# A two-layer hybrid attention trunk: weight blocks loaded two blocks ahead, measured on two engines, and the first x tiles normalised through PE

## The chip, the cores and the metric

The kernel runs on one core of a Trainium2 chip. A time is the device time of one execution in microseconds (us), and the time of a kernel is the median of its runs. Five engines work beside each other, each through its own instructions in their order: PE (matrix multiplications; "PEld" is the loading of its stationary operand), DVE (vector engine), ACT (scalar engine), POOL (GpSimd) and SP (which here only issues DMA transfers). An instruction that waits for data holds up everything behind it on its engine, and only that.

## What is computed

One sequence of 1024 rows, 1024 features and 16 heads of 64 goes through two layers of the form x + W_out(mixer(RMSNorm(x)) * silu(gate)). Layer 0 is causal attention with a forget gate ("fox"), layer 1 is windowed attention at three dilations, merged by a softmax over their log-sums ("dsw").

```python
D_MODEL, SEQ, DEPTH, HEAD_DIM, N_HEADS = 1024, 1024, 2, 64, 16
DSWA_GROUPS = ((128, 1), (512, 4), (2048, 16))      # window, dilation

def rms_norm(x, g):
    return x * lax.rsqrt(jnp.mean(x * x, axis=-1, keepdims=True) + EPS) * g

def fox_mixer(h, w_in, b_f, q_g, k_g):
    # proj = h @ w_in: q, k, v, gate of 1024 columns each, and 16 forget logits
    q, k = rms_norm(q, q_g), rms_norm(k, k_g)       # by head
    c = jnp.cumsum(jax.nn.log_sigmoid(f_logit + b_f), axis=1)
    # s = q k^T / 8 + c[query] - c[key], causal; o = softmax(s) v
    return o, gate

def dsw_mixer(h, cos, sin, w_in, q_g, k_g):
    # proj = h @ w_in: q, k, v for 3 groups x 16 heads (9216 columns) and a gate (1024)
    # q, k: rms_norm by head, rotary on 16 of the 64 features
    # per group: attention inside its window on every r-th row; o_g and lse_g
    return sum(softmax(lse over groups) * o_g), gate

# layer: x = x + (o * silu(gate)) @ w_out
```

## The kernel before

**Tiles and precision.** The 1024 rows are 8 tiles of 128. Every large product is made of three fp16 matmuls: an operand is held as a high and a low half, and high x high, high x low and low x high are summed. `xh`, `xl` hold the normalised input of a layer, turned so that its features lie on the partitions, and `yh`, `yl` the gated output of the mixer. The fp32 weights come from memory in 44 blocks of mostly 1024 x 384: 3 gate blocks, 8 fox blocks (q, k and v of two heads), 3 output blocks of layer 0; then 3 gate blocks, 24 dsw blocks (8 of dilation group 0, then groups 2 and 1 in turn), 3 output blocks of layer 1.

**One block's weights** (class `Weights`). A block is four pieces of 2 x 384 columns on 128 partitions, and four steps are done to each: `load` (a DMA on SP's queue into one of four `raw` buffers), `bound` (L270: DVE takes the largest absolute value of each partition, `vm`), `scale` (once per block: PE's small matmul L248 adds the squares of these over the partitions, and a chain of one-column operations on DVE makes a power of two `sw` of it, with `eps` and the factors `col`, `vs` for v), and `split` into the fp16 halves `w`. The split has two forms: on ACT and DVE (L300, L301: the high half by ACT, the remainder by DVE) or on POOL with a cast on ACT (L303, L304, L305). Pieces 1 and 3 go the first way, pieces 0 and 2 the second.

**Order.** PE's order is the order in which the program is written: for each of the eight tiles of a block `project` (L328, 24 matmuls into one of three `pj` buffers in PSUM), with attention work of earlier tiles between. The clock of that order is `Flow`: `project` ticks four times a tile, so a block has 32 ticks, and `flow.at(slot, ...)` writes a piece of work at a tick. `Weights.ahead()` puts the work on the next block into the present one: loads at ticks 2, 4, 6 and 9, bounds at 8, 10, 12, 15, the scale at 20, splits at 21, 23, 25, 27. On the other engines a scheduler arranges the instructions when the program is built; the ticks only tell it where a piece of work may begin. At run time each engine and SP's queue keep that fixed order.

**One tile after its projection.** DVE multiplies q and k by their gains out of `pj` (`u`, L410), ACT squares them (L415), ACT and DVE move v out as fp16 halves (`vt`, L420, L421); for each pair of tiles DVE makes the norms (L428, L451, L452, L454), ACT and POOL split q and k into halves (`hl`, L456, L457), and SP issues the transposing DMA into `qk_t` (L462). PE makes scores `s` (L482) from it, DVE and ACT the probabilities `p`, ACT and POOL their halves `ph` (L528, L531 in fox), another transposing DMA makes `ptt`, and PE multiplies with v (L539).

**Start.** x comes in twice: turned (`xt`, L554) and by rows (`xrow`). `row_factor` (L563 to L570) gets 1/rms of a tile's rows on ACT and DVE from the rows, puts it on a diagonal `dg`, and `split_xt` lets PE spread it over the partitions (L578) and multiplies and splits the turned tile. `load_gbc` reads the norm's gains as one row for every partition and takes their largest for the scale `sx`. The loads stand on SP's queue in the order row 0, gains, x 0, weights 0 and 1, gains as rows, weights 2 and 3, row 1, x 1, row 2, x 2.

Of the kernel before, what the change touches and what calls it, by code (L numbers as in the profile page):

```python
# [22 lines left out]
P = 128  # L23
D = 1024
# [12 lines left out]
CB = 2  # L37
PARTS = ((0, 384), (384, 256), (640, 384))
# [44 lines left out]
def trunk(ctx, tc, ins, out, cfg):  # L83
# [59 lines left out]
    xh, xl, yh, yl = (const.tile([P, KT, S], F16, name=n) for n in ("xh", "xl", "yh", "yl"))  # L143
# [81 lines left out]
    sx = const.tile([P, 2], F32, name="sx")  # L225
    sy = const.tile([P, 2], F32, name="sy")
# [8 lines left out]
    def root_floor(e, q, lo, hi):  # L235

        nc.vector.tensor_scalar(e, q, 1, 0x7FC00000, ALU.logical_shift_right, ALU.bitwise_and)
        nc.vector.tensor_scalar(e, e, float(127 << 22), None, ALU.add)
        nc.vector.tensor_single_scalar(e, e, 0x7F800000, ALU.bitwise_and)
        nc.vector.tensor_scalar(e, e, float((127 + lo) << 23), float((127 + hi) << 23), ALU.max, ALU.min)  # L240

    def spread_sums(src, n):
# [7 lines left out]
        nc.vector.tensor_reduce(v1, ws, AX.X, ALU.add)  # L250
        return v1
# [4 lines left out]
    class Weights:  # L256


        def __init__(self, src, n, layer, kind):
            self.src, self.n, self.layer, self.kind = src, n, layer, kind  # L260
            self.raw, self.pairs = {}, {}
            self.vm = sm.tile([P, KT // 2], F32, name="vm", tag="vm")
            self.vm2 = sm.tile([P, KT // 2], F32R, name="vm2", tag="vm2")

        def load(self, i):
            self.raw[i] = w_p.tile([P, 2, 384], F32, name="raw", tag="raw", bufs=4)
            nc.sync.dma_start(self.raw[i][:, :, : self.n], self.src[:, 2 * i : 2 * i + 2, :])

        def bound(self, i):
            nc.vector.tensor_reduce(self.vm[:, i : i + 1], self.raw[i][:, :, : self.n], AX.XY, ALU.max, apply_absolute_value=True)  # L270
            if i == KT // 2 - 1:
                nc.vector.tensor_mul(self.vm2, self.vm, self.vm)

        def scale(self):

            v1 = spread_sums(self.vm2, KT // 2)
            e = v1.bitcast(I32)
            root_floor(e, e, -16, 40)
            f = self.f = sm.tile([P, 6], F32, name="ws_f", tag="ws_f")
            sw, t2, inv = (f[:, i : i + 1] for i in range(3))  # L280
            self.sw, self.inv = sw, inv
            nc.vector.tensor_scalar(sw.bitcast(I32), e, -1.0, float(268 << 23), ALU.mult, ALU.add)  # L282
            by = sy if self.kind == "out" else sx
            nc.vector.tensor_mul(t2, sw, by[:, self.layer : self.layer + 1])
            nc.vector.reciprocal(inv, t2)
            if self.kind != "qkv":
                return
            self.eps, self.col, self.vs = (f[:, i : i + 1] for i in range(3, 6))
            nc.vector.scalar_tensor_tensor(self.eps, t2, EPS, t2, ALU.mult, ALU.mult)
            nc.vector.tensor_scalar(self.col, t2, 2.0 ** -15, 2.0 ** -14, ALU.mult, ALU.max)  # L290
            nc.vector.tensor_scalar(self.col, self.col, 2.0 ** 15, None, ALU.min)
            nc.vector.tensor_mul(self.vs, self.col, inv)
            lw = low[:, self.layer : self.layer + 1]
            nc.vector.tensor_tensor(lw, lw, sw, ALU.min)

        def split(self, i, own=False):
            raw, n = self.raw[i][:, :, : self.n], self.n
            w = self.pairs[i] = w_p.tile([P, 2, 2, 384], F16, name="w", tag="w", bufs=cfg["wbufs"])
            if own or (cfg["wl"][self.layer] >> i) & 1:
                nc.scalar.activation(w[:, 0, :, :n], raw, AF.Copy, scale=self.sw)  # L300
                nc.vector.scalar_tensor_tensor(w[:, 1, :, :n], raw, self.sw, w[:, 0, :, :n], ALU.mult, ALU.subtract)  # L301
            else:
                nc.gpsimd.tensor_scalar(raw, raw, self.sw, None, ALU.mult)  # L303
# [6 lines left out]
        def ahead(self):  # L310

            s0 = flow.now
            for i in range(KT // 2):
                flow.at(s0 + cfg["wload"][i], lambda i=i: self.load(i))
# [834 lines left out]
```

## Time and profile before

| | |
|---|---|
| median of 3 runs | 1936.68 us (1935.25 to 1941.52) |
| profiled execution | 1936.61 us |
| its span, first to last instruction | 1934.7 us |
| mean granted TensorE clock | 0.953 |
| busy: PE, DVE | 1688.3 (87%), 1318.4 (68%) |
| busy: POOL, ACT | 1081.7 (56%), 1010.9 (52%) |
| DMA engines, bytes moved by the queues | 66.4%, 292.54 MB on the hardware queue |

A span's busy time says how much an engine worked, not whether its work was waited for; for that the profile lists the idle time in front of an instruction and what ended it ("53.4 <- DMA" reads: 53.4 us of idle time that a DMA's landing ended). Lines in it such as `L270 DVE TENSOR_REDUCE vm<-raw` name the line of the kernel, the engine, the operation, and the program's names of what is written and read. The stages can be told by time: PE's first projection starts at 32.3 us, the fox blocks take some 60 us each, the 24 dsw blocks some 41 us each.

### The profile page before, as it was taken

How to read it: one execution, taken by the hardware profiler on the slowest of the kernel's cores; microseconds unless marked ns; L12 is line 12 of the kernel's file. 1: busy time of each engine (PE TensorE's matmuls, PEld its weight loads, DVE VectorE, ACT ScalarE, POOL GpSimd, SP SyncE). 2: the span in 40 equal slices, each digit the busy share in tenths (PEclk: the TensorE clock that was granted, in tenths of full speed). 3: DMA queues.
4: the chain of work that ended last, by engine and by line, in shares of the span. 5: the costliest groups of instructions: out<-in, count | busy, mean ns of one | idle time of the engine just before them, and what ended most of it. 6: DMA issues, size and time to landing. Idle time of an engine off the chain costs nothing.

```text
span 1934.7 us, 38039 instructions
## 1 busy us (share of the span) xinstructions
PE 1688.3 (87%) x13308; PEld 1071.8 (55%) x13308; DVE 1318.4 (68%) x4089; ACT 1010.9 (52%) x2492; POOL 1081.7 (56%) x1105
## 2 busy tenths in 40 slices
PE   3898888988888888998999989998988889998889
PEld 2655565655665434755666555555555555555544
DVE  8776676666756668676666686666766766767762
ACT  5545566555665445545555565544554554554620
POOL 4324566455654463255667656666676666767531
PEclk9999999988989998999999999999999999999999
DMA  7244977889879767246667686576565756567752
GB/s 250 93 159 97 186 172 152 162 169 182 167 147 193 207 207 220 89 122 138 130 138 141 143 189 132 133 146 130 132 134 140 165 129 139 139 145 149 184 160 88
DMA packets 659344, 294.96 MB, mean 152 GB/s; under 512 B 510272, under 2 KB 622912, under 8 KB 659152
## 3 DMA queue, kind: packets, MB, share of 16 engines
q1 hardware_dynamic: 659152, 292.54, 66.4%
q8 instruction: 104, 1.70, 0.4%
q14 instruction: 88, 0.72, 0.1%
HBM read 126.45 MB, written 41.22 MB: 87 GB/s over the span
## 4 chain that ended last, share of the span: by engine, by line
PE 25%; DMA 17%; DVE 15%; issue 5%; ACT 5%; POOL 4%; SPq 1%; DVEq 0%; ACTq 0%; POOLq 0%
PE pj L328 17%; DMA qk_t<-hl 6%; DMA raw<-in_w_dsw 6%; PE pj L352 5%; DVE w L301 3%; DMA ptt<-ph 2%; PE s L482 2%; DVE vm L270 2%; DVE p L943 1%; DMA og_d<-og 1%; ACT p L944 1%; DVE pj L428 1%; DVE u L410 1%; DMA raw<-in_w_do 1%; DVE u L454 1%
## 5 line engine op out<-in xcount | busy, mean ns | idle before, releaser
L328 PE MATMUL pj<-w,xh 128*128 128x384 f16 (+2 forms) x4864 | 1212.9, 334 | 55.5 <-DVE vt L421 43.3
L328 PE MATMUL pj<-w,xl 128*128 128x384 f16 (+2 forms) x2432 | 809.8, 333 | 9.2 <-DVE xl L864 7.8
L328 PEld LDWEIGHTS <-xh 128*128 128x128 f16 x4864 | 480.4, 101 | 353.6 <-issue 90.0
L328 PEld LDWEIGHTS <-xl 128*128 128x128 f16 x2432 | 244.4, 101 | 180.8 <-issue 23.7
L531 POOL TENSOR_TENSOR ph<-p,ph 128x512 f16<-128x512 f32 (+3 forms) x176 | 175.1, 1012 | 189.6 <-ACT ph L528 157.5
L303 POOL TENSOR_SCALAR raw<-raw,ws_f 128x768 f32<-128x768 f32 (+2 forms) x86 | 184.2, 2151 | 116.1 <-DVE ws_f L282 113.2
L482 PE MATMUL s<-qk_t 128*128 128x128 f16 (+1 forms) x1504 | 168.2, 255 | 91.6 <-DMA qk_t<-hl 82.8
L457 POOL TENSOR_TENSOR hl<-u,hl 128x512 f16<-128x512 f32 x128 | 151.6, 1184 | 164.6 <-ACT hl L456 145.3
L270 DVE TENSOR_REDUCE vm<-raw 128x1 f32<-128x768 f32 (+2 forms) x176 | 161.7, 921 | 100.1 <-DMA raw<-in_w_dsw 71.1
L415 ACT ACTIVATE sq<-pj 128x256 f32<-128x256 f32 x256 | 96.8, 378 | 225.5 <-DVE u L410 214.3
L949 POOL TENSOR_TENSOR ph<-p,ph 128x768 f16<-128x768 f32 (+2 forms) x96 | 153.8, 1602 | 87.3 <-ACT ph L948 85.5
L482 PEld LDWEIGHTS <-qk_t 128*128 128x128 f16 x1504 | 117.3, 101 | 110.8 <-DMA qk_t<-hl 91.5
L352 PE MATMUL pj<-yh,w 128*128 128x512 f16 x512 | 161.8, 386 | 1.0 <-POOL w L305 1.0
L305 POOL TENSOR_TENSOR w<-raw,w 128x768 f16<-128x768 f32 (+2 forms) x86 | 148.3, 1729 | 4.2 <-ACT w L304 4.2
L456 ACT CAST hl<-u 128x512 f16<-128x512 f32 x128 | 79.1, 618 | 133.2 <-DMA qk_t<-hl 82.7
L525 ACT ACTIVATE p<-p,acc 128x512 f32<-128x512 f32 (+2 forms) x192 | 109.1, 608 | 74.5 <-DVE acc L707 73.1
L410 DVE TENSOR_TENSOR u<-pj,gr 128x256 f32<-128x256 f32 x256 | 106.6, 416 | 56.5 <-PE pj L328 56.0
L301 DVE SCALAR_TENSOR_TENSOR w<-raw,ws_f,w 128x768 f16<-128x768 f32 (+2 forms) x90 | 121.6, 1353 | 33.4 <-ACT w L300 33.4
L539 PEld LDWEIGHTS <-ptt 128*128 128x128 f16 x1136 | 108.4, 100 | 52.1 <-DMA ptt<-ph 39.8
L421 DVE SCALAR_TENSOR_TENSOR vt<-pj,ws_f,vt 128x128 f16<-128x128 f32 x256 | 89.1, 348 | 59.1 <-ACT vt L420 58.0
L352 PEld LDWEIGHTS <-w 128*128 128x128 f16 x768 | 75.3, 100 | 87.5 <-issue 6.7
L528 ACT CAST ph<-p 128x512 f16<-128x512 f32 (+3 forms) x176 | 87.4, 535 | 55.8 <-DMA ptt<-ph 55.0
(194 smaller groups left out, 2903.2 us busy)
## 6 DMA issues: line engine op xcount, KB each, us to landing
raw<-in_w_dsw SPq DMA_DIRECT2D x96, 384.0 KB, 3.7
raw<-in_w_fox SPq DMA_DIRECT2D x32, 384.0 KB, 4.0
og_d<-og SPq DMA_DIRECT2D x64, 132.0 KB, 2.8
cmb<-og_d SPq DMA_DIRECT2D x64, 132.0 KB, 2.4
bc<-c_d SPq DMA_DIRECT2D x32, 256.0 KB, 4.0
gs_d<-ge SPq DMA_DIRECT2D x32, 192.0 KB, 2.2
xrow<-in_x SPq DMA_DIRECT2D x8, 512.0 KB, 5.5
xt<-in_xt SPq DMA_DIRECT2D x16, 256.0 KB, 4.8
```

The lines of the kernel that those rows point to most:

```text
L270: nc.vector.tensor_reduce(self.vm[:, i : i + 1], self.raw[i][:, :, : self.n], AX.XY, ALU.max, apply_absolute_value=True)
L301: nc.vector.scalar_tensor_tensor(w[:, 1, :, :n], raw, self.sw, w[:, 0, :, :n], ALU.mult, ALU.subtract)
L303: nc.gpsimd.tensor_scalar(raw, raw, self.sw, None, ALU.mult)
L305: nc.gpsimd.tensor_sub(w[:, 1, :, :n], raw, w[:, 0, :, :n])
L328: nc.tensor.matmul(ps[:, :n], a[:, k, cols], w.slab(k, j), start=(k == 0 and i == 0), stop=(k == KT - 1 and i == 2))
L352: nc.tensor.matmul(ps[m], w.slab(k, j)[:, m * P : (m + 1) * P], a[:, k, 512 * b : 512 * (b + 1)], start=(k == 0 and x == 0), stop=(k == KT ...
L410: nc.vector.tensor_mul(u[:, t % 2].rearrange("p (a b) d -> p a b d", a=2), ps[:, : 4 * HD].rearrange("p (a b d) -> p a b d", a=2, b=2), gr ...
L457: nc.gpsimd.tensor_sub(hl[:, :, :4, 1], u, hl[:, :, :4, 0])
L482: nc.tensor.matmul(s[:, c0 : c0 + cnt * P].rearrange("p (c s) -> p c s", c=cnt), qk[:, i, blk], kk[:, j : j + cnt, e], start=(h == 0), sto ...
L525: nc.scalar.activation(p, p, AF.Exp, bias=acc, scale=-1.0)
L531: (nc.gpsimd if pool_l else nc.vector).tensor_sub(ph[:, e, 1, cols], p, ph[:, e, 0, cols])
L949: nc.gpsimd.tensor_sub(ph[:, 1], st["p"], ph[:, 0])
```

## The change

- **Loads.** `raw` has eight buffers instead of four, and the blocks stand in one list, `blocks`. While block i runs, `next_block` loads block i + 2 (ticks 18, 20, 22, 24) and measures, scales and splits block i + 1.
- **Measuring** moves to the first ticks of a block (0, 1, 3, 4). Pieces 0 and 2 are reduced by DVE (L281) as before; pieces 1 and 3 are squared and summed by ACT (L279), which with that does for two of four pieces what DVE did.
- **Scale** moves from tick 20 to 8 and has fewer operations: v is moved out with a constant factor `VS` in place of `vs`, so `col` and `vs` go, and `eps` is made by ACT.
- **Splits** move from ticks 21 to 27 to ticks 10, 16, 22 and 12. Pieces 0, 1 and 2 are split by ACT and DVE (L310, L311), and only piece 3 by POOL with ACT's cast (L313 to L315).
- **Start.** The loads stand in the order x 0, gains, the four pieces of weights, x 1, row 2, x 2, and behind them the four pieces of block 1. For x tiles 0 and 1 `column_factor` takes the factor from the turned tile: ACT squares it, eight fp32 matmuls with ones (L605) sum over the features, and a short chain on DVE and ACT makes 1/rms on all partitions at once. Rows 0 and 1 aren't loaded. `gain_scale` replaces `load_gbc`: the largest gain of each partition is transposed by PE (L400), reduced, and spread by a matmul (L402).
- **Memory.** `yh`, `yl` are now the same tiles as `xh`, `xl`.

Counted over the program, DVE has 183 instructions fewer (3908 for 4091), ACT 212 more (2698 for 2486), POOL 86 fewer (1024 for 1110), SP issues four loads fewer, and PE has 18 instructions more.

The diff, cut to this (small changes of signatures are left out):

```diff
-    xh, xl, yh, yl = (const.tile([P, KT, S], F16, name=n) for n in ("xh", "xl", "yh", "yl"))
+    xh, xl = (const.tile([P, KT, S], F16, name=n) for n in ("xh", "xl"))
+    yh, yl = xh, xl
...
         def load(self, i):
-            self.raw[i] = w_p.tile([P, 2, 384], F32, name="raw", tag="raw", bufs=4)
+            self.raw[i] = w_p.tile([P, 2, 384], F32, name="raw", tag="raw", bufs=cfg["rbufs"])
...
         def bound(self, i):
-            nc.vector.tensor_reduce(self.vm[:, i : i + 1], self.raw[i][:, :, : self.n], AX.XY, ALU.max, apply_absolute_value=True)
...
+            raw = self.raw[i][:, :, : self.n]
+            if i % 2:
+                jk = sb.tile([P, 2, self.n], F16, name="jk", tag="jk", bufs=1)
+                nc.scalar.activation(jk, raw, AF.Square, accum_out=self.vm[:, i : i + 1])
+            else:
+                nc.vector.tensor_reduce(self.vm[:, i : i + 1], raw, AX.XY, ALU.max, apply_absolute_value=True)
             if i == KT // 2 - 1:
-                nc.vector.tensor_mul(self.vm2, self.vm, self.vm)
+                v = [a.rearrange("p (a b) -> p a b", b=2) for a in (self.vm, self.vm2)]
+                nc.scalar.activation(v[1][:, :, 0], v[0][:, :, 0], AF.Square)
+                nc.scalar.copy(v[1][:, :, 1], v[0][:, :, 1])
...
-            self.eps, self.col, self.vs = (f[:, i : i + 1] for i in range(3, 6))
-            nc.vector.scalar_tensor_tensor(self.eps, t2, EPS, t2, ALU.mult, ALU.mult)
-            nc.vector.tensor_scalar(self.col, t2, 2.0 ** -15, 2.0 ** -14, ALU.mult, ALU.max)
-            nc.vector.tensor_scalar(self.col, self.col, 2.0 ** 15, None, ALU.min)
-            nc.vector.tensor_mul(self.vs, self.col, inv)
...
+                nc.scalar.activation(self.eps, t2, AF.Square, scale=EPS ** 0.5)
...
         def split(self, i, own=False):
...
-            if own or (cfg["wl"][self.layer] >> i) & 1:
+            if own or i != cfg["wpool"]:
                 nc.scalar.activation(w[:, 0, :, :n], raw, AF.Copy, scale=self.sw)
                 nc.vector.scalar_tensor_tensor(w[:, 1, :, :n], raw, self.sw, w[:, 0, :, :n], ALU.mult, ALU.subtract)
...
+    def next_block():
+
+        i, s0 = upto[0], flow.now
+        upto[0] += 1
+        for j in range(KT // 2):
+            if i + 2 < len(blocks):
+                flow.at(s0 + cfg["wload"][j], lambda j=j: blocks[i + 2].load(j))
+            if i + 1 < len(blocks):
+                flow.at(s0 + cfg["wbound"][j], lambda j=j: blocks[i + 1].bound(j))
+                flow.at(s0 + cfg["wsplit"][j], lambda j=j: blocks[i + 1].split(j))
+        if i + 1 < len(blocks):
+            flow.at(s0 + cfg["wscale"], blocks[i + 1].scale)
+        return blocks[i]
...
-        nc.scalar.activation(vt[:, t, :, HD : 2 * HD], pv, AF.Copy, scale=vs)
+        nc.scalar.activation(vt[:, t, :, HD : 2 * HD], pv, AF.Copy, scale=VS)
...
-    def load_gbc(layer):
-        gbc = lay([P, D], F32, name="gbc", tag="ph")
-        nc.sync.dma_start(gbc, norm_g[layer].partition_broadcast(P))
-        gm = sm.tile([P, 1], F32, name="gm", tag="gm")
-        nc.vector.tensor_reduce(gm, gbc, AX.X, ALU.max, apply_absolute_value=True)
...
+    def gain_scale(layer, g):
+
+        gm = sm.tile([P, 2], F32, name="gm", tag="gm")
+        nc.vector.tensor_reduce(gm[:, 0:1], g, AX.X, ALU.max, apply_absolute_value=True)
+        pt = ps_s.tile([P, 512], F32, name="pg", tag="s")
+        nc.tensor.transpose(pt[:1, :P], gm[:, 0:1], ident)
+        nc.vector.tensor_reduce(gm[:1, 1:2], pt[:1, :P], AX.X, ALU.max)
+        nc.tensor.matmul(pt[:, P : P + 1], ones[:1].bitcast(F32), gm[:1, 1:2], start=True, stop=True)
...
+    def column_factor(t):
+
+        sq = lay([P, D], F32, name="xsq", tag="ptt")
+        nb = ps_s.tile([P, 512], F32, name="nb", tag="s")
+        for h in range(2):
+            nc.scalar.activation(sq[:, 512 * h : 512 * (h + 1)], xts[t, h], AF.Square)
+            for k in range(4 * h, 4 * h + 4):
+                nc.tensor.matmul(nb[:, :P], ones.bitcast(F32), sq[:, k * P : (k + 1) * P], start=(k == 0), stop=(k == KT - 1))
+        v, a, y = (nb[:, i * P : (i + 1) * P] for i in (1, 2, 3))
+        r = sm.tile([P, P], F32, name="dg", tag="dg", bufs=2)
+        nc.vector.tensor_scalar(v, nb[:, :P], 1.0 / D, EPS, ALU.mult, ALU.add)
+        nc.scalar.activation(r, v, AF.Ln)
+        nc.scalar.activation(r, r, AF.Exp, scale=-0.5)
...
-    load_row(0)
+    load_xt(0)
     nc.sync.dma_start(gt, ins["norm_gt"])
-    load_xt(0)
-    w.load(0)
-    w.load(1)
-    load_gbc(0)
-    w.load(2)
-    w.load(3)
-    load_row(1)
+    for i in range(KT // 2):
+        w.load(i)
     load_xt(1)
     load_row(2)
     load_xt(2)
...
-wload=(2, 4, 6, 9), wbound=(8, 10, 12, 15), wscale=20, wsplit=(21, 23, 25, 27))
+wload=(18, 20, 22, 24), wbound=(0, 1, 3, 4), wscale=8, wsplit=(10, 16, 22, 12))
```

(The last two lines are the ends of the table `CFG`, which also gains `rbufs=8` and `wpool=3` and loses `wl=(0xA, 0xA)`.)

How the change moves instructions is seen in the order in which they stand on an engine. A row names the line, the operation, what is written and read with buffer numbers, and the tile's size.

DVE before, where one dsw block gives way to the next: `vm` measures the next block, `w` is the last splits, `u` and `vt` read the projections of the tiles at the boundary.

```order
L301 SCALAR_TENSOR_TENSOR w_13920<-raw_13594,ws_f_13882,w_13920 128x768
L421 SCALAR_TENSOR_TENSOR vt_13565<-pj_13897,ws_f_13293,vt_13565 128x2x64
L410 TENSOR_TENSOR u_14039<-pj_14007,gr_111 128x256
L270 TENSOR_REDUCE vm_14152<-raw_14169 128x1
L301 SCALAR_TENSOR_TENSOR w_14030<-raw_13713,ws_f_13882,w_14030 128x768
L421 SCALAR_TENSOR_TENSOR vt_13565<-pj_14007,ws_f_13293,vt_13565 128x2x64
L451 SCALAR_TENSOR_TENSOR pj_13897<-pj_13897,rs_v_13984 128x8
L410 TENSOR_TENSOR u_14039<-pj_14045,gr_111 128x256
L452 SCALAR_TENSOR_TENSOR pj_13897<-pj_13897,rs_y_13994 128x8
L270 TENSOR_REDUCE vm_14152<-raw_14183 128x1
```

Here a measuring stands between two splits and ahead of an eviction of `vt` from `pj`. DVE after, in a dsw block's second to fourth tile:

```order
L311 SCALAR_TENSOR_TENSOR w_14371<-raw_13930,ws_f_14325,w_14371 128x768
L474 SCALAR_TENSOR_TENSOR pj_14243<-pj_14243,rs_v_14335 128x8
L444 SCALAR_TENSOR_TENSOR vt_14200<-pj_14358,vt_14200 128x2x64
L475 SCALAR_TENSOR_TENSOR pj_14243<-pj_14243,rs_y_14345 128x8
L477 TENSOR_TENSOR u_14237<-u_14237,pj_14243 128x512
L311 SCALAR_TENSOR_TENSOR w_14477<-raw_13944,ws_f_14325,w_14477 128x768
L433 TENSOR_TENSOR u_14390<-pj_14396,gr_109 128x256
L311 SCALAR_TENSOR_TENSOR w_14556<-raw_13965,ws_f_14325,w_14556 128x768
```

and behind eight rows of score work, which follow the last of these, come the measurings of the block after next:

```order
L281 TENSOR_REDUCE vm_15447<-raw_15142 128x1
L451 TENSOR_REDUCE pj_14396<-sq_14391 128x8
L481 COPY hl_14351<-hl_14351 128x2x256
L281 TENSOR_REDUCE vm_15447<-raw_15185 128x1
L453 TENSOR_SCALAR rs_v_14483<-pj_14396,ws_f_13736 128x8
```

The three splits have moved from the block's end to its first half, and both measurings of DVE stand together behind them. `raw_15142` has the buffer that `raw_13930` had, which the first split frees. SP's queue after, at the same place, holds the loads of that block between the transposes:

```order
L270 DMA raw_15142<-in_w_dsw 128x768
L270 DMA raw_15158<-in_w_dsw 128x768
L270 DMA raw_15185<-in_w_dsw 128x768
L1083 DMA og_d_89<-og_14146 128x2x132
L270 DMA raw_15231<-in_w_dsw 128x768
L485 DMA_TRANSPOSE qk_t_14356<-hl_14351 128x12x128
```

Before, the loads stood likewise three and one between the transposes, but were those of the next block; now they are those of the block after it. PE's first rows, before and then after:

```order
L248 MATMUL ws<-vm_131,ones 128x4
L578 MATMUL nb<-dg,ones 128x128 x3
L328 LDWEIGHTS xh
L328 MATMUL pj<-w,xh 128x384
L328 LDWEIGHTS xh
```

```order
L400 MATMUL pg<-ident,gm 1x128
L402 MATMUL pg<-gm,ones 128x1
L605 MATMUL nb<-xsq,ones 128x128 x8
L252 MATMUL ws<-vm_194,ones 128x4
L605 MATMUL nb<-xsq,ones 128x128 x8
L595 MATMUL nb<-dg,ones 128x128
L345 LDWEIGHTS xh
```

Of the three factors that PE spreads ahead of its first projection, two are now sums over the turned tiles, and one still comes from rows.

174 lines of the change are left out of this document (86 added, 88 removed).

## The prediction

> **What bounds the kernel now.** I read the busy time by stage first, then PE's waits in the two long stages, then one block's beginning in the chain that ended last. By stage (columns: window, its length, then busy time of PE, PEld, DVE, ACT and POOL with the number of instructions, granted clock, DMA share, GB/s):
>
> ```profile
> 0.00:32.30 32.30, 2.37 (x7) 1.74 (x8) 25.57 (x69) 15.32 (x31) 11.20 (x18) 1.00 0.89 319
> 164.00:526.00 362.00, 303.48 (x2982) 209.81 (x2982) 243.56 (x794) 212.59 (x498) 207.34 (x180) 0.92 0.81 164
> 794.00:1834.00 1040.00, 938.23 (x7316) 598.00 (x7314) 723.02 (x2432) 550.53 (x1501) 666.10 (x755) 0.96 0.65 141
> ```
>
> The first row is the start, before PE's projections; the second holds six attention blocks of layer 0 (fox), the third the 24 dilated blocks of layer 1 (dsw) and what lies around them. PE is busy 90% of the dsw stage and 84% of the fox stage, no other engine over 70%: the kernel runs at PE's pace plus PE's waits. Those are, in dsw (first two) and fox (last two), in us in total, times, longest:
>
> ```profile
> PE s L482 <- DMA qk_t<-hl: 53.4, 22, 5.1
> PE pj L328 <- DVE vt L421: 42.8, 23, 3.5
> ...
> PE o L539 <- DMA ptt<-ph: 34.1, 12, 5.4
> PE s L482 <- DMA qk_t<-hl: 29.5, 8, 6.9
> ```
>
> Per dsw block that is 96.2 / 24 = 4.0 us in two waits, one where a new weight block begins (L328) and one some 9 us later (L482). The chain through one block's beginning shows the cause:
>
> ```profile
> 1061.56 0.94 ACT w L300
> 1062.53 1.03 DVE w L301
> 1063.57 2.97 DMA raw<-in_w_dsw
> 1066.57 0.06 DVE vm L270
> 1066.62 0.81 issue
> 1067.44 2.04 DVE w L301
> 1069.48 0.27 DVE vt L421
> 1069.79 5.26 PE pj L328 x21
> ```
>
> DVE works in order. Its measuring of the next block's weights (vm) stands ahead of a split (w) and of the eviction (vt) behind which PE waits. It waits for a load that could start only when the split at 1062.53 had emptied one of the four raw buffers. In the dsw stage DVE's waits of this kind are:
>
> ```profile
> DVE vm L270 <- DMA raw<-in_w_dsw: 71.1, 39, 3.7
> DVE w L301 <- ACT w L300: 19.9, 19, 2.1
> ```
>
> A wait of PE costs clock too. After one of 3.39 us, two matmuls take 0.85 us instead of 0.49, and likewise after one of 3.06 us at a block's beginning:
>
> ```profile
> 1111.49 0.49 PE L328 MATMUL pj<-w,xh 128*128 128x384 f16 x2
> ...
> 1121.93 1.89 PE L482 MATMUL s<-qk_t 128*128 128x128 f16 x12 [3.39 <-DMA qk_t<-hl]
> ...
> 1124.57 0.85 PE L328 MATMUL pj<-w,xh 128*128 128x384 f16 x2
> ...
> 1325.44 0.48 PE L328 MATMUL pj<-w,xh 128*128 128x384 f16 x2 [3.06 <-DVE vt L421]
> ...
> 1326.00 0.85 PE L328 MATMUL pj<-w,xh 128*128 128x384 f16 x2
> ```
>
> At a mean of 0.96 the dsw stage loses 0.04 x 1040 = 42 us to it, part of that inside the waits themselves.
>
> **The change, part by part.** The prices are these groups (busy us, mean ns of one, idle before):
>
> ```profile
> L303 POOL TENSOR_SCALAR raw<-raw,ws_f 128x768 f32<-128x768 f32 x78 | 171.5, 2208 | 109.5 <-DVE ws_f L282 109.5
> L270 DVE TENSOR_REDUCE vm<-raw 128x1 f32<-128x768 f32 x160 | 150.9, 945 | 96.7 <-DMA raw<-in_w_dsw 71.1 <-DMA raw<-in_w_fox 11.9 <-DMA raw<-in_w_gate 6.1
> L305 POOL TENSOR_TENSOR w<-raw,w 128x768 f16<-128x768 f32 x78 | 138.1, 1774 | 2.6 <-ACT w L304 2.6
> L301 DVE SCALAR_TENSOR_TENSOR w<-raw,ws_f,w 128x768 f16<-128x768 f32 x82 | 114.3, 1396 | 28.5 <-ACT w L300 28.5
> L300 ACT ACTIVATE w<-raw,ws_f 128x768 f16<-128x768 f32 x82 | 76.0, 930 | 0.0
> L304 ACT CAST w<-raw 128x768 f16<-128x768 f32 x78 | 64.2, 823 | 24.9 <-POOL raw L303 24.5
> L289 DVE SCALAR_TENSOR_TENSOR ws_f<-ws_f 128x1 f32<-128x1 f32 x32 | 22.6, 706 | 0.0
> L566 ACT ACTIVATION_READ_ACCUMULATOR xrow<-xrow 128x1 f32 x8 | 1.5, 186 | 0.0
> ```
>
> *DVE, per block:* two reductions fewer (-1.89 us), one split more (+1.40; ends 1.03 and 2.04, the two in the chain above), L289 gone to ACT (-0.71), three more one-column operations gone (an estimate of -0.9; ends 0 and three times L289's price). That is -2.1 us. The raw wait is 71.1 / 24 = 3.0 us a block now. Eight buffers do not end it: buffer and load are released by the split of two blocks earlier, and in the new order DVE's measurings stand right behind those splits. Ends 0 and 3.0. I take 1.0: ahead of the first measuring stand two further splits, four score operations and more, over 5 us, while a load lands in some 3 us in the chain; ahead of the second only some 3 us. Together 4.1 us less on DVE per block, all of it away from the block's beginning, since scale and splits now stand at the second to third tile and no weight work at the last two.
>
> *ACT, per block:* two squares with accumulator, 2 x (0.93 + 0.19), priced by the split activation and the accumulator read since no row has a square of this shape; a split instead of a cast (+0.11); some three small operations (+0.6). That is +2.95 us, 130 us over 44 blocks. ACT's 550.53 of 1040 us hide it on average, but it comes in a lump of 3 x 0.93 + 0.82 + 2.24 = 5.9 us. Behind it are queued the squares and copies that read PE's projections and the exponentials; DVE's evictions wait for these. Its ends are 0 and 2.95 us a block.
>
> *Sum for dsw:* PE's waits per block could fall by 4.0 (all) or by 0. DVE's 4.1 less would cover all of them; against it stands ACT's lump, of which I let 1.9 us reach PE, two thirds of 2.95. So 24 x 2.1 = -50 us. Of the clock's 42 us the same share (2.1 of 4.0) is 22; as part lies inside waits I take half, -11 (ends 0 and -22).
>
> [...]
>
> *Fox.* POOL loses one L303 and one L305 per block (-3.98 us). Here that is on the path: two L303 in a row hold up the split of p, whose transposed copy PE then waits for:
>
> ```profile
> 266.95 4.38 POOL L303 TENSOR_SCALAR raw<-raw,ws_f 128x768 f32<-128x768 f32 x2
> ...
> 275.61 1.20 POOL L531 TENSOR_TENSOR ph<-p,ph 128x512 f16<-128x512 f32 x1
> ...
> 278.78 0.24 PE L539 MATMUL o<-vt,ptt 128*128 128x65 f16 x1 [4.79 <-DMA ptt<-ph]
> ```
>
> I take half of the 34.1 us (-17) and leave the 29.5 for qk_t, since its transposes stand behind ACT's and POOL's work as before. ACT's 2.95 us lands in a stage with ACT at 59% (212.59 of 362); a quarter of 7 x 2.95 is +5. Net -12, ends -34 and +21.
>
> *Start.* Weights are measured by 13.4, and PE's first projection stands in its order behind a factor of the third x tile that DVE makes last:
>
> ```profile
> 12.48 0.95 DVE L270 TENSOR_REDUCE vm<-raw 128x1 f32<-128x768 f32 x1
> 24.23 1.93 DVE L301 SCALAR_TENSOR_TENSOR w<-raw,ws_f,w 128x768 f16<-128x768 f32 x2
> 31.74 0.80 PE L578 MATMUL nb<-dg,ones 128*128 128x128 f32 x2 [11.22 <-DVE dg L570]
> 32.32 0.85 PE L328 MATMUL pj<-w,xh 128*128 128x384 f16 x2
> ```
>
> Ahead of the last weight load stand 0.5 MB of x now instead of 1.5 MB of x, rows and gains: at 319 GB/s 3 us sooner. The other row load and gain pass leave DVE (3 to 6 us of what stands between 26.2 and 31.7). New are 16 matmuls of 128 columns, 0.4 us each by the pair at 31.74, half of them ahead of the weights' scale but beside its loads. I take -7, ends 0 and -10.
>
> *The rest* at zero: a lone x buffer for both halves of a layer makes the writers of y wait for x's last readers, but each tile's columns are projected before y is written to them; if that cover is gone, each of the two output projections waits one eviction, under 1 us. Gate and output blocks: ends -10 and +5.
>
> Sum: -50 - 11 - 12 - 7 = -80, from the profiled execution's 1936.6 us (span 1934.7), which equals the median of 1936.68: **1857 us**.
>
> **The rivals.** *The loads are no earlier where it counts.* For it: the release by the splits, told above. Then the 3.0 us stay on DVE, and ACT's squares wait as well. Of dsw only 24 x 0.8 = 19 remain (2.1 us less burst, less most of ACT's lump), with start and fox 38: 1899. *All waits of dsw vanish.* For it: DVE's 4.1 us match PE's 4.0. Then 96 + 22 + 12 + 7 = 137: 1800. *ACT takes over as the bound, slower.* Squares that wait for loads as DVE's reductions did (71.1 / 39 = 1.8 us each) make its lump 5.9 + 3.6 = 9.5 us. Once it passes two tiles of PE's work (10 us, what PE's three PSUM buffers allow), its 2.95 us come through in 31 blocks, +91, against -7 at the start and 24 x 2.1 = -50 from DVE: 1971. Against it: ACT idles 47% of dsw. *No change:* qk_t's transposes, which PE waits for longest, stay as late as now, and what DVE saves is lost to them: 1937.
>
> **How the numbers follow.** Forecast 0.54, loads no earlier 0.20, all vanish 0.11, ACT the bound 0.10, no change 0.05. A measurement here can tell 0.3% (5.8 us) from no change. Faster: 0.54 + 0.11 + 0.19 = 0.84; same 0.06; slower 0.10. The range runs from the case of no waits, 1800, past the 1899 of the late loads to 1918, and leaves out ACT's case and no change.
>
> **What would show it.** Right: first projection near 25 us; in dsw DVE's wait for raw near 24 us and PE's waits near 45 to 50, the L328 one nearly gone; POOL busy some 175 us less, ACT 130 more; granted clock in dsw 0.97. Wrong: PE waiting at the third or fourth tile of a block for DVE or ACT, ACT's squares or DVE's vm waiting over 60 us for raw, or fox blocks no shorter.

## The result, and the profile after

The changed kernel takes 1819.15 us, the median of 4 runs (1813.33 to 1825.56), against 1939.07 for the kernel before, measured beside it: a ratio of 0.9384, 95% interval 0.9344 to 0.9424. The forecast was 1857 in a range of 1800 to 1918, a gain of 80 us; 120 came. The profiled execution took 1813.33 us with a span of 1811.5, 123.2 us less than before. The stages, cut at the starts of PE's first projections (worked out from the two traces, us; the forecast is the sum's term for the stage, in dsw the waits and the clock together):

| stage | before | after | difference | forecast |
|---|---|---|---|---|
| start, to the first projection | 32.3 | 23.7 | -8.6 | -7 |
| three gate blocks | 97.2 | 105.3 | +8.1 | 0 |
| seven fox blocks | 396.5 | 360.7 | -35.8 | -12 |
| last fox block, output | 193.5 | 189.9 | -3.6 | 0 |
| gate blocks of layer 1 | 106.0 | 104.1 | -1.9 | 0 |
| 24 dsw blocks | 1010.4 | 933.4 | -77.0 | -61 |
| output | 98.8 | 94.4 | -4.4 | 0 |

The busy times of the page after:

```profile
PE 1659.2 (92%) x13342; PEld 1060.2 (59%) x13342; DVE 1259.9 (70%) x3906; ACT 1068.3 (59%) x2790; POOL 872.5 (48%) x1019
```

The fox and dsw stages by window (columns as in the prediction; the windows of dsw end a little before the stage does), before

```profile
129.50:526.00 396.50, 335.81 (x3185) 229.17 (x3183) 268.88 (x864) 227.01 (x537) 219.75 (x188) 0.93 0.78 161
825.50:1833.90 1008.40, 906.82 (x7122) 579.11 (x7120) 701.13 (x2388) 534.99 (x1473) 656.81 (x750) 0.96 0.66 142
```

and after:

```profile
129.10:489.80 360.70, 325.82 (x3184) 222.49 (x3183) 248.93 (x821) 228.66 (x584) 183.20 (x172) 0.97 0.81 172
783.80:1716.60 932.80, 885.35 (x7132) 571.06 (x7130) 677.49 (x2273) 567.42 (x1641) 534.28 (x704) 0.98 0.72 153
```

Between these two windows of dsw 75.6 us went. PE's matmuls are the same, yet its busy time fell by 21.5 us, since the granted clock rose from 0.96 to 0.98; the other 54 us are waits. Those left in dsw after are these:

```profile
ACT jk L279 <- DMA raw<-in_w_dsw: 34.1, 30, 3.2
...
PE s L505 <- DMA qk_t<-hl: 24.5, 23, 4.7
...
PE pj L345 <- DVE vt L444: 18.1, 9, 2.9
...
DVE vm L281 <- DMA raw<-in_w_dsw: 7.1, 9, 1.3
```

PE's two waits went from 96.2 us to 42.6, DVE's wait for weights from 71.1 to 7.1, and ACT, which now measures half of the pieces, waits 34.1 for them instead. DVE's timeline in the second tile of a dsw block and what follows shows the new order at work (the four rows left out are the rest of one pair's norms and an eviction, the later ones scores):

```profile
946.30 1.70 DVE L300 TENSOR_TENSOR low<-low,ws_f 128x1 f32<-128x1 f32 x1
947.93 0.28 DVE L444 SCALAR_TENSOR_TENSOR vt<-pj,vt 128x128 f16<-128x128 f32 x1
948.13 0.41 DVE L433 TENSOR_TENSOR u<-pj,gr 128x256 f32<-128x256 f32 x1
948.46 1.22 DVE L311 SCALAR_TENSOR_TENSOR w<-raw,ws_f,w 128x768 f16<-128x768 f32 x1
...
950.74 1.65 DVE L311 SCALAR_TENSOR_TENSOR w<-raw,ws_f,w 128x768 f16<-128x768 f32 x1
952.32 0.41 DVE L433 TENSOR_TENSOR u<-pj,gr 128x256 f32<-128x256 f32 x1
952.65 1.57 DVE L311 SCALAR_TENSOR_TENSOR w<-raw,ws_f,w 128x768 f16<-128x768 f32 x1
...
955.52 0.94 DVE L281 TENSOR_REDUCE vm<-raw 128x1 f32<-128x768 f32 x1
```

Evictions stand between the splits, and the measuring (955.52) starts without idle time in front of it. The first row is odd: one column of 128 values takes 1.70 us. It comes back below.

### The profile page after: what moved, and what is told of

The parts are those of the page before. It is cut to its first block, busy times and chain, and to the rows that moved or that the text cites. A ratio compares the mean times of both kernels' runs of the same rounds, so it can differ in the third digit from the quotient of the medians.

```text
span 1811.5 us, 38107 instructions
## 1 busy us (share of the span) xinstructions
PE 1659.2 (92%) x13342; PEld 1060.2 (59%) x13342; DVE 1259.9 (70%) x3906; ACT 1068.3 (59%) x2790; POOL 872.5 (48%) x1019
## 4 chain that ended last, share of the span: by engine, by line
PE 36%; DVE 12%; DMA 11%; POOL 5%; issue 5%; ACT 3%; SPq 0%; DVEq 0%; POOLq 0%; ACTq 0%
PE pj L345 24%; PE pj L369 8%; DMA qk_t<-hl 6%; PE s L505 2%; DMA raw<-in_w_dsw 2%; DVE p L970 2%; DVE w L311 2%; DVE hl L481 1%; POOL hl L480 1%; POOL ph L976 1%; DVE pj L451 1%; POOL cmb L1003 1%; DMA ptt<-ph 1%; DVE vm L281 1%; POOL raw L313 1%
## 5 line engine op out<-in xcount | busy, mean ns | idle before, releaser
L345 PE MATMUL pj<-w,xh 128*128 128x384 f16 (+2 forms) x4864 | 1191.2, 329 | 32.7 <-DVE vt L444 18.3
L345 PE MATMUL pj<-w,xl 128*128 128x384 f16 (+2 forms) x2432 | 799.1, 329 | 4.8 <-DVE xl L898 2.6
L345 PEld LDWEIGHTS <-xh 128*128 128x128 f16 x4864 | 473.8, 99 | 322.5 <-issue 48.1
L345 PEld LDWEIGHTS <-xl 128*128 128x128 f16 x2432 | 241.4, 99 | 166.7 <-issue 10.6
L480 POOL TENSOR_TENSOR hl<-u,hl 128x512 f16<-128x512 f32 x128 | 153.9, 1203 | 131.5 <-ACT hl L479 131.3
L976 POOL TENSOR_TENSOR ph<-p,ph 128x768 f16<-128x768 f32 (+2 forms) x96 | 154.0, 1604 | 119.4 <-ACT ph L975 116.1
L505 PE MATMUL s<-qk_t 128*128 128x128 f16 (+1 forms) x1504 | 162.9, 249 | 51.2 <-DMA qk_t<-hl 40.1
L311 DVE SCALAR_TENSOR_TENSOR w<-raw,ws_f,w 128x768 f16<-128x768 f32 (+2 forms) x133 | 181.5, 1379 | 9.6 <-ACT w L310 9.5
L369 PE MATMUL pj<-xh,w 128*128 128x512 f16 x512 | 162.0, 386 | 0.0
L444 DVE SCALAR_TENSOR_TENSOR vt<-pj,vt 128x128 f16<-128x128 f32 x256 | 73.3, 289 | 109.1 <-ACT vt L443 107.1
L438 ACT ACTIVATE sq<-pj 128x256 f32<-128x256 f32 x256 | 96.2, 376 | 76.7 <-DVE u L433 68.0
L310 ACT ACTIVATE w<-raw,ws_f 128x768 f16<-128x768 f32 (+2 forms) x133 | 116.9, 911 | 13.7 <-DVE ws_f L293 13.7
L279 ACT ACTIVATE jk<-raw 128x768 f16<-128x768 f32 (+2 forms) x88 | 72.3, 821 | 85.5 <-DMA raw<-in_w_dsw 43.6
L465 POOL TENSOR_TENSOR ra<-u,cs 128x128 f32<-128x128 f32 x96 | 50.3, 524 | 148.7 <-DVE u L433 69.8
L433 DVE TENSOR_TENSOR u<-pj,gr 128x256 f32<-128x256 f32 x256 | 106.2, 415 | 17.2 <-PE pj L345 16.9
```

The source lines that it names most:

```text
L345: nc.tensor.matmul(ps[:, :n], a[:, k, cols], w.slab(k, j), start=(k == 0 and i == 0), stop=(k == KT - 1 and i == 2))
L369: nc.tensor.matmul(ps[m], w.slab(k, j)[:, m * P : (m + 1) * P], a[:, k, 512 * b : 512 * (b + 1)], start=(k == 0 and x == 0), stop=(k == KT ...
L433: nc.vector.tensor_mul(u[:, t % 2].rearrange("p (a b) d -> p a b d", a=2), ps[:, : 4 * HD].rearrange("p (a b d) -> p a b d", a=2, b=2), gr ...
L438: nc.scalar.activation(sq[:, t % 2], ps[:, : 4 * HD], AF.Square)
L480: nc.gpsimd.tensor_sub(hl[:, :, :4, 1], u, hl[:, :, :4, 0])
L505: nc.tensor.matmul(s[:, c0 : c0 + cnt * P].rearrange("p (c s) -> p c s", c=cnt), qk[:, i, blk], kk[:, j : j + cnt, e], start=(h == 0), sto ...
```

## The experiments

Every ratio is against runs of the kernel before on the same chip. What a run gives back is counted from the changed kernel's 1819 us; where the interval of its ratio overlaps the changed kernel's, 0.9344 to 0.9424, it is hard to tell from none. Stage lengths are from each run's trace. All runs made from the changed kernel also keep one detail of its diff that neither the words of the change nor the sum had looked at: POOL's scaling in `split` (L313) has a second factor, 1.0. It matters, and is taken up under order_old_scale.

**four_raw**: are the eight buffers the cause?

```diff
-rbufs=8, wload=(18, 20, 22, 24)
+rbufs=4, wload=(18, 20, 23, 24)
```

> The changed kernel with four raw buffers instead of eight (and the third piece's load at tick 23 instead of 22); all else stays, and DVE's order is the same. Theory O (the order: measurings and splits no longer stand ahead of the evictions at a block's boundary): 1820, 1808 to 1832, waits of PE in dsw near 45 us as in the changed kernel. Theory B (the buffers: loads that start earlier): measurings wait for loads some 70 us again and dsw gives back 40 to 76 us: 1860 to 1895.

1823.51 us, ratio 0.942 (0.9388 to 0.9452), which cannot be told from the changed kernel. Waits in dsw:

```profile
ACT jk L279 <- DMA raw<-in_w_dsw: 38.6, 26, 3.8
...
PE s L505 <- DMA qk_t<-hl: 33.1, 25, 5.4
...
PE pj L345 <- DVE vt L444: 15.8, 9, 2.6
DVE vm L281 <- DMA raw<-in_w_dsw: 10.6, 13, 1.4
```

Theory B falls: the second four buffers are worth at most a few us (dsw 941.2 us for 933.4). What they do is seen in the traces. The weights of the eighth dsw block, which is projected from 1046.8 us on in four_raw and from 1046.9 in the changed kernel, are loaded from 987.8 us in four_raw and from 949.7 in the changed kernel: two blocks ahead with four buffers and three, not two, with eight. (The program writes this load into the block that begins at 971.1 us in the changed kernel; the scheduler has put it ahead of that, so a tick holds no load back.) In either kernel the loads follow the splits that free their buffers, and the measuring follows the loads.

**ticks_alone**: is the place of the weight work the cause?

```diff
-wload=(2, 4, 6, 9), wbound=(8, 10, 12, 15), wscale=20, wsplit=(21, 23, 25, 27)
+wload=(0, 0, 0, 0), wbound=(0, 1, 3, 4), wscale=8, wsplit=(10, 16, 22, 12)
```

> The kernel before with the ticks of its weight work changed and nothing else: loads at tick 0, bounds at 0, 1, 3, 4, scale at 8, splits at 10, 16, 22, 12; four raw buffers, loads one block ahead. Theory O: within 15 us of order_alone, 1870 (1850 to 1890), L328's wait at the boundary nearly gone. Theories B and W: 1925 to 1945, since neither buffers nor work have changed.

1937.93 us, ratio 0.9992 (0.9963 to 1.0022): nothing. Yet the wait that the prediction had named is gone in dsw:

```profile
PE s L482 <- DMA qk_t<-hl: 75.7, 41, 5.2
...
DVE vm L270 <- DMA raw<-in_w_dsw: 57.4, 45, 5.5
...
PE ob L539 <- DMA ptt<-ph: 17.0, 8, 5.2
...
PE pj L328 <- DVE vt L421: 1.3, 1, 1.3
```

L328's wait fell from 42.8 us to 1.3, while those for the transposes rose from 53.4 to 75.7 and from none to 17.0. Theory O, that the place alone makes the gain, falls: what was freed at the boundary was lost some tiles later. The place is not quite that of the changed kernel, though: here the loads start at the block's first tick, directly ahead of the measuring, and DVE still waits 57.4 us for them.

**pool_alone**: does POOL's work matter?

```diff
-wl=(0xA, 0xA)
+wl=(0x7, 0x7)
```

> The kernel before with pieces 0, 1 and 2 split by ACT and DVE and only piece 3 by POOL, at the old ticks. Fox should gain 15 to 30 us from POOL's two L303 in a row. In dsw DVE has a third split at the boundary. Theory O: dsw loses about one split a block, 24 x 1.4 = 34, so 1940 (1925 to 1960) in all. Theory W (POOL's work was the brake): dsw no worse, 1905 to 1920.

1910.81 us, ratio 0.985 (0.9819 to 0.9881): a gain of 27, but not where it was expected. Fox is unchanged (398.3 us for 396.5): its waits for ptt fell and those for qk_t rose. Dsw became 37 us shorter (973.1 us), although DVE has a split more at the boundary:

```profile
PE s L482 <- DMA qk_t<-hl: 48.9, 23, 5.3
...
DVE vm L270 <- DMA raw<-in_w_dsw: 41.3, 33, 2.6
...
PE pj L328 <- DVE vt L421: 24.5, 13, 4.1
```

DVE's wait for loads fell from 71.1 us to 41.3. A likely reason, which no run isolates: POOL's way over a piece takes 2.2, 0.8 and 1.8 us one after the other, that of ACT and DVE 0.9 and 1.2, so that a buffer comes free sooner. Of the gain 15 us were lost again in the first gate blocks and in the stage of the last fox block and its output.

**two_on_pool**: the same part undone in the changed kernel.

```diff
-            if own or i != cfg["wpool"]:
+            if own or i % 2:
```

> The changed kernel with pieces 0 and 2 split by POOL again (1 and 3 by ACT and DVE); all else stays. pool_alone gained 37 us in dsw and nothing in fox. Theory P (POOL's long splits hold up its halves of q, k and p, for which PE's transposes wait): 1852 (1840 to 1865), most of the loss in dsw as waits for qk_t. Theory O (order and measuring): DVE has a split less, 1819 or faster (1805 to 1825).

1833.70 us, ratio 0.9458 (0.9428 to 0.9488): 15 us back, of them 16 in dsw, where the wait for qk_t is 49.7 us instead of 24.5. The direction of theory P, less than half of its size.

**all_on_dve**: the squares of ACT undone.

```diff
-            if i % 2:
+            if False:
...
-                nc.scalar.activation(v[1][:, :, 0], v[0][:, :, 0], AF.Square)
-                nc.scalar.copy(v[1][:, :, 1], v[0][:, :, 1])
+                nc.vector.tensor_mul(self.vm2, self.vm, self.vm)
```

> The changed kernel with all four pieces measured by DVE; all else stays. Theory M (ACT takes the waits for loads off DVE as well as two reductions): DVE's waits for raw in dsw back from 7 to some 35 us or more, its work up 24 x 1.9 = 45 us, and PE's waits up by about half of both: 1850 (1838 to 1870). Theory P (POOL alone was the brake in dsw): under 10 us more, 1819 to 1829.

1829.71 us, ratio 0.9438 (0.9406 to 0.947): 11 us back, at the edge of the noise, of them 5 in dsw. DVE was busy 716 us there instead of 678, and hardly waited for loads:

```profile
PE s L503 <- DMA qk_t<-hl: 29.6, 22, 6.1
...
PE pj L343 <- DVE vt L442: 16.4, 9, 3.2
...
DVE vm L281 <- DMA raw<-in_w_dsw: 4.5, 10, 1.3
```

So it isn't ACT's help that ended DVE's wait, and 38 us more work on DVE cost PE 5: theory M falls.

**old_start**: the order of loads, `row_factor` for all x tiles and `load_gbc` put back.

```diff
-    load_xt(0)
+    load_row(0)
     nc.sync.dma_start(gt, ins["norm_gt"])
+    load_xt(0)
...
-    nb = column_factor(0)
+    row_factor(0)
...
-    split_xt(0, nb)
+    split_xt(0, spread_factor(0))
```

> The changed kernel with the old start (rows 0 and 1, gains as rows, factors of x tiles 0 and 1 from rows); all else stays. The first projection came 8.6 us sooner but the three gate blocks took 8.2 us longer. If the two belong together: 1820 (1812 to 1828), first projection near 32 us, gate blocks near 97. If the new start is worth its 8.6 us: 1828 or more.

1822.88 us, ratio 0.9401 (0.9341 to 0.946). First projection at 30.6 us, gate blocks 98.5 for 105.3: the start's gain is given back in the block behind it, as the first reading expected. After the change PE's longest waits from 23 to 105 us are these:

```profile
PE nb L595 <- DVE dg L590: 9.5, 1, 9.5
PE pj L345 <- DVE ge L536: 5.7, 3, 4.5
...
PE nb L595 <- DVE nv L587: 4.8, 1, 4.8
```

The first of them, for the third x tile's factor, ends at 23.2 us, ahead of the first projection, and belongs to the start. Behind one tile of projections PE waits another 4.8 us, for the factor of the fourth x tile, which like the third's still comes from rows; the old start has no such wait. At 61.4 us it waits 4.5 us for a gate's eviction, where the kernel before waits 3.4 in all for these. With its clock at 0.95 in the gate blocks instead of 0.98 PE is also busy 2.5 us longer there.

**order_alone, order_four_raw, order_old_scale** take parts away in turn: first POOL's share, ACT's squares and the new start (order_alone), then also four of the eight buffers (order_four_raw), then also the new scale (order_old_scale, which has `reciprocal`, `eps` on DVE, `col` and `vs` as before).

```diff
 order_alone: two_on_pool, all_on_dve and old_start together
 order_four_raw: also
-rbufs=8, wload=(18, 20, 22, 24)
+rbufs=4, wload=(18, 20, 23, 24)
 order_old_scale: also the edit of undo_scale (below)
```

> The changed kernel with three parts undone: two of four pieces split by POOL, all four measured by DVE, the old start. What stays of the change is the place of the weight work, the eight buffers and the shorter scale. Theory O: dsw keeps two thirds or more of its 76 us, fox a third of its 36: 1865, 1850 to 1885. Theory W (the gain comes from the work taken off DVE and POOL): waits of PE in dsw back over 80 us, 1905 to 1935.

> order_alone with four raw buffers: against ticks_alone it has the shorter scale, the constant factor of v and one tile for x and y, and the loads later. Theory S (the shorter scale and the constant VS make the 68 us between ticks_alone and order_alone): 1872 (1858 to 1885). Theory B (buffers do it where DVE still measures all): 1900 or more.

> order_four_raw with the old scale and the old factors of v (reciprocal, eps by DVE, col, vs) put back. Against ticks_alone it then has only the loads after the splits instead of at tick 0, and one tile for x and y. Theory S (the shorter scale and the constant factor of v made the 56 us): 1930 (1915 to 1945). Theory L (the place of the loads made them): 1890 or less (1870 to 1895).

Measured: 1869.54 (0.9644, 0.962 to 0.9667), 1881.54 (0.9707, 0.9659 to 0.9755) and 1900.18 us (0.9801, 0.9765 to 0.9837). The first two are where the theories of the order and of the scale had them, the first by luck: its dsw stage kept 33 of 77 us and not two thirds, its fox stage 34 of 36 and not a third. The third lies between its two theories. Undoing the scale cost 19 us here, and 38 remain to ticks_alone that neither theory covers. In that gap lie the place of the loads, one tile for x and y, and POOL's second factor, in ticks_alone

```profile
L303 POOL TENSOR_SCALAR raw<-raw,ws_f 128x768 f32<-128x768 f32 x78 | 171.6, 2212 | 116.8 <-DVE ws_f L282 75.2 <-DVE v L239 21.4 <-DMA c_d<-fc 20.2
```

and in order_old_scale:

```profile
L312 POOL TENSOR_SCALAR raw<-raw,ws_f 128x768 f32<-128x768 f32 x78 | 70.1, 911 | 123.9 <-DVE ws_f L291 99.7 <-DVE v L242 24.2
```

The instruction takes 911 ns instead of 2212, 101 us of POOL's time for 78 pieces of this size. pool_alone gained 27 us by taking 155 us from POOL (1081.7 to 926.6); in that proportion 101 us would be worth 18, an estimate and about half of the 38. The factor by itself wasn't tried, so how the 38 us divide stays open.

**undo_scale**: the new scale undone in the changed kernel.

```diff
-                nc.vector.tensor_scalar(t2, self.sw, by[:, ly], 2.0, ALU.mult, ALU.max)
...
-                nc.scalar.activation(self.eps, t2, AF.Square, scale=EPS ** 0.5)
...
+            nc.vector.tensor_mul(t2, sw, by[:, self.layer : self.layer + 1])
...
+            nc.vector.scalar_tensor_tensor(self.eps, t2, EPS, t2, ALU.mult, ALU.mult)
...
+            nc.vector.tensor_mul(self.vs, self.col, inv)
...
-        nc.scalar.activation(vt[:, t, :, HD : 2 * HD], pv, AF.Copy, scale=VS)
+        nc.scalar.activation(vt[:, t, :, HD : 2 * HD], pv, AF.Copy, scale=vs)
```

> The changed kernel with the old scale and the old factors of v put back; all else stays. The small operations cost DVE 33 us more over the program and the evictions of v 59 ns more each, 256 times, 15 us. Theory S: at least these 48 us come back, 1867 or more (1855 to 1880). Theory L: it costs what DVE's own work costs when half hidden, 1835 (1822 to 1845).

1901.13 us, ratio 0.9796 (0.9765 to 0.9826): 82 us back, all of them in dsw (1026.2 us for 933.4); fox stays at 358.0. The smallest-looking part is the dearest to take away. PE's waits in dsw:

```profile
PE s L506 <- DMA qk_t<-hl: 56.9, 25, 5.0
PE pj L346 <- DVE vt L445: 47.8, 16, 4.1
```

DVE in a dsw block of this run:

```profile
966.99 0.76 DVE L300 SCALAR_TENSOR_TENSOR ws_f<-ws_f 128x1 f32<-128x1 f32 x1
967.67 0.14 DVE L301 TENSOR_SCALAR ws_f<-ws_f 128x1 f32<-128x1 f32 x1
967.85 0.15 DVE L302 TENSOR_SCALAR ws_f<-ws_f 128x1 f32<-128x1 f32 x1
968.04 1.82 DVE L303 TENSOR_TENSOR ws_f<-ws_f 128x1 f32<-128x1 f32 x1
969.78 2.48 DVE L312 SCALAR_TENSOR_TENSOR w<-raw,ws_f,w 128x768 f16<-128x768 f32 x1
972.18 0.41 DVE L434 TENSOR_TENSOR u<-pj,gr 128x256 f32<-128x256 f32 x1
972.52 0.34 DVE L445 SCALAR_TENSOR_TENSOR vt<-pj,ws_f,vt 128x128 f16<-128x128 f32 x1
972.77 1.93 DVE L312 SCALAR_TENSOR_TENSOR w<-raw,ws_f,w 128x768 f16<-128x768 f32 x2
975.71 0.95 DVE L281 TENSOR_REDUCE vm<-raw 128x1 f32<-128x768 f32 x1 [1.00 <-DMA raw<-in_w_dsw]
976.58 0.34 DVE L445 SCALAR_TENSOR_TENSOR vt<-pj,ws_f,vt 128x128 f16<-128x128 f32 x1
```

From DVE's first small operation behind the scale's matmul to its last, a block takes 5.7 us instead of 3.8 (means over the dsw blocks). Four of them have two tensor inputs (in this kernel's lines L295, L300, L303 and L305) and take 2.5 us together; the changed kernel has one of this kind, at 0.8. And no eviction stands between the last of them and the first split. An eviction of `vt` then ends 14.5 us behind its projection, 9.9 in the changed kernel (medians of the fourth tile in the first eight dsw blocks). With three `pj` buffers PE stops two tiles, some 10 us, after a projection that isn't evicted. The first eight blocks gave 50 us back. The other sixteen gave 43, and there the same eviction ends 9.9 us behind instead of 9.4, so this account doesn't cover them.

**scale_tile_later**: is it the order that undo_scale changed?

```diff
-wscale=8, wsplit=(10, 16, 22, 12)
+wscale=12, wsplit=(14, 20, 25, 16)
```

> The changed kernel with the scale at tick 12 instead of 8, so that its matmul on PE stands one tile later, and the splits at 14, 20, 25 and 16. Instructions and work are the same, but DVE's order in a dsw block is then that of undo_scale: the first measuring directly behind the last two splits and ahead of the evictions of v, where the changed kernel has an eviction between the splits and four score operations ahead of the measuring. Theory Q (it is this order that cost undo_scale its 93 us in dsw, not the work of the old scale): 1880 (1860 to 1915), dsw over 980 us with waits of PE for vt at the third to fifth tile. Theory W (the work): 1819 (1810 to 1830), dsw 933.

1825.87 us, ratio 0.9414 (0.9368 to 0.9459): 7 us more, 11 in dsw (944.0 us), with the evictions of that tile 12.7 us behind. Theory Q falls: by itself this order costs little. That leaves the work that undo_scale put back, which is of two kinds: the longer chain of the scale, and slower evictions of v (ACT's part 357 ns instead of 267, DVE's 349 instead of 289). Together they make 40 us more of DVE's busy time in dsw (718 for 678). PE's clock was at half rate for 95.6 us in dsw instead of 30.7, which costs some 32 us of work and follows from the waits. The two make 72 of the 93 us, and all_on_dve bore 38 us more on DVE for a price of 5; so it matters where on DVE the time is put, and the sum is no proof. No run undoes the scale without the factor of v, so how the 93 us divide between them stays open.

**four_raw_two_hl**: a try for more.

```diff
-hb=1, rbufs=8
+hb=2, rbufs=4
```

> four_raw with two hl buffers instead of one; hl is the split of q and k that the transposing DMA reads. In the changed kernel ACT waits 86 us in dsw for such a transpose before it may write the next hl, and PE's remaining waits there are for qk_t and for ACT's part of vt. If this wait of ACT is what PE still waits for: dsw 20 to 35 us shorter, 1795 (1785 to 1805). If it is only idle time that ACT has anyway: 1820 (1810 to 1830).

1815.44 us, ratio 0.9354 (0.9318 to 0.9391): not to be told from the changed kernel. ACT's wait for the transposes was idle time that it had anyway.

## Why the prediction was right in sum, and where it wasn't

By stages the forecast of 80 us is 43 short of the 123 between the two traces: 24 in fox, 16 in dsw, 10 in later stages put at zero and 2 at the start, less the 8 that the first gate blocks lost.

**The waits of PE in dsw** were the right place and the right size: 2.1 us a block were forecast, 53.6 / 24 = 2.2 came. The reason given for it was only half right, and that the size came out so well is in part luck. The term for loads (DVE's wait from 3.0 to 1.0 us a block) was credited to earlier measuring with more slack, and the slack is there; but four_raw shows that the buffers have hardly a share in it (DVE's wait is 10.6 us there, 7.1 in the changed kernel), all_on_dve that ACT has none either, and ticks_alone that without the other parts the new place gains nothing. The rival "no change" was what ticks_alone did: the transposes took what DVE saved.

**The scale's small operations** were the mis-sized step. The sum had 1.61 us a block for them, 0.71 for L289 and an estimate of 0.9 for three more. As DVE's busy time that was too much: `low` became the operation that is held up (754 ns instead of 179), and over the program the small operations behind the root took DVE 22 us less, 33 with the squaring that went to ACT. As a part of the change it was too little: undone together with the constant factor of v, which the sum had at nothing, they cost 82 us. L289's 706 ns for one column stood in the profile and should have been asked about. It is a wait: 28 of its 32 instances take 0.70 to 0.76 us and end 0.90 to 0.92 us behind the start of POOL's L303, and the one that falls into the late part of an L303 takes 0.13. And it stands in the one chain that the splits, and the evictions behind them, stand behind.

**POOL** was priced in fox only and at nothing in dsw. In fox half of the wait for ptt was to go, and half went: 33.4 us became 16.9 (the prediction's 34.1 and 29.5 are counted to 586 us, beyond the stage's end at 526). In dsw pool_alone and two_on_pool show 37 and 16 us. L303 was carried over at 2208 ns, while in the changed kernel it takes 961.

**Fox** gave 36 us, not 12. The wait for qk_t, left as it was, fell from 24.7 to 11.2 us, ACT's +5 did not come (its busy time there went from 227.0 to 228.7 us), and the sum had no clock term for the stage, though its granted clock went from 0.93 to 0.97 and PE was busy 10 us less for it. Why the wait for qk_t fell is not shown: in pool_alone, with POOL's part alone, it rose to 31.8 us.

**The clock** in dsw gave 21.5 us of PE's busy time, not 11: its upper end of 22. Halving it because part would lie inside the waits was wrong; the half rate follows the wait (below).

**ACT** gained 57 us of busy time, not 130. The evictions of v with a constant factor take 267 ns instead of 357, 256 times, 23 us that the sum left out. Its instructions add up to 94 us more; neighbouring records overlap, so the busy time rose less. The sum let 1.9 us a block of ACT's lump reach PE. Most of the remaining wait for vt, 18.1 us in 9 waits, looks like it: it stands ahead of the seventh tile of every other one of the last sixteen blocks, which takes the `pj` buffer of the fourth, and ACT's part of the fourth tile's eviction ends some 10 us behind its projection there, 8 in the other blocks. But all_on_dve, without ACT's squares, has the same wait in the same tiles (16.4 us in 9), so the squares aren't its cause. The rival in which ACT becomes the bound would have made all_on_dve faster than the changed kernel; it is 11 us slower.

**The start** came 8.6 us sooner, and the sum missed that the block behind it gives that back. **The last fox block, the gate blocks of layer 1 and the output blocks**, put at zero, gave 10 us.

## What to carry to other kernels

Undo the parts of a change one at a time in the new kernel and do them one at a time in the old: here they gave 4, 15, 11, 4 and 82 us back when undone, of which the two of 4 can't be told from none and 11 barely can, while the ticks and POOL's share gave 0 and 27 when done alone, so that no part has a price of its own. An instruction that takes many times what others of its size take (706 ns for one column, where its neighbours take 150) may be a wait in disguise; ask whose instruction its end goes with before pricing it at its mean. And when a wait in front of an in-order engine's work is removed, look for the next one in the same block before counting the gain.

## What the runs showed of the hardware

**DVE's and POOL's instructions hold each other up in these traces.** POOL's timeline of the changed kernel at the place of the odd row above:

```profile
945.86 2.13 POOL L976 TENSOR_TENSOR ph<-p,ph 128x1024 f16<-128x1024 f32 x1
947.97 0.90 POOL L313 TENSOR_SCALAR raw<-raw,ws_f 128x768 f32<-128x768 f32 x1
```

DVE's `low` (946.30 to 948.00) ends when POOL's L976 ends (947.99). Of its 32 instances in the changed kernel five take 0.15 us, and each of the 27 longer ones, 0.27 to 1.70 us, ends within 17 ns of the end of an instruction of POOL. In undo_scale DVE's L303 (to 969.86) ends with POOL's `ph` likewise:

```profile
967.71 2.13 POOL L977 TENSOR_TENSOR ph<-p,ph 128x1024 f16<-128x1024 f32 x1
```

In the changed kernel DVE's splits take 1.00 us while POOL is idle and up to 2.39 beside it; the reductions of the same pieces take 0.92 to 0.95 either way. DVE's operations held up in the two traces read two operands from SBUF (`low`, the splits), but for one, the copy of `hl` (L481, fp16 from SBUF to SBUF): 0.26 to 0.30 us while POOL is idle, up to 1.53 beside it. `u<-u,pj` (L477), one of whose operands lies in PSUM, takes 0.67 to 0.69 us either way. POOL is held up likewise: 107 of its 128 L480 (`hl<-u,hl`) in the changed kernel take 1.15 to 1.17 us, the other 21 take 1.31 to 1.95, and 20 of these 21 have a split of DVE (L311) beside them. `low` is held up to the end of POOL's instruction, L289 in the kernel before for only some 0.91 us of the 2.2 that POOL's L303 lasts. So a part of the new scale's worth, by these times, is that it has one operation of two tensor inputs in place of four: in 22 dsw blocks the four take 56.1 us of DVE's time in undo_scale, the one 19.9 in the changed kernel.

**POOL's scaling took less than half the time with a second factor of 1.0**: 911 ns in the mean of order_old_scale, 916 in two_on_pool and 961 in the changed kernel, against 2207 in pool_alone, 2208 in the kernel before and 2212 in ticks_alone, which have no second factor, all at 128x768. Why isn't known from these runs.

**The clock kept to a grid in these traces.** In the kernel before and the changed one all changes of the granted clock lie whole multiples of 3.41 us apart, and it is 1.0 or 0.5. Over the traces of all 14 kernels, from the first projection on, of the grid's windows at full rate in which PE idled over 60%, 326 of 326 were followed by a window at half rate; below 45% none of 6420 were; between, 55 of 207. In the two traces alone it was 50 of 50, none of 905 and 9 of 39. So a wait of 2.1 us, 60% of 3.41, was followed by the half rate each time that it fell into one window, and not always when two shared it: in the changed kernel PE idled for 3.37 us from 1281.92 on, across the border of two windows at 1283.42, and the clock stayed at 1.00. A window of the changed kernel in which PE idled 74% (no matmul or weight load), and the one behind it:

```profile
327.66:331.07 3.41, 0.90 (x24) 0.78 (x24) 1.20 (x4) 0.83 (x3) 0.67 (x1) 1.00 1.08 224
331.07:334.49 3.42, 2.87 (x13) 1.78 (x14) 2.25 (x9) 2.28 (x8) 0.29 (x1) 0.51 0.79 176
```
